# Order of the retrieval entries behind the projections: blocks 4 and 5 run their best experts into their lists, blocks 6 and 7 take theirs along with their lists

## The chip, the cores and the metric

The kernel runs on 1 core of one Trainium2 chip. The metric is the device time of one execution in microseconds. Three timed runs of the kernel before took 1407.05, 1413.61 and 1411.08 us, median 1411.08.

## The reference, cut to what matters

One decoder block over 1024 tokens of 1024 channels in float32. A gated linear attention branch and a chunked gating branch share one input projection; they are merged, projected back and added to x. Behind them stands a mixer of experts, on which the change works:

```python
h2 = modulate(rms_norm(x, norm2_w), shift2, scale2)
q = (h2 @ w_q)                        # 8 heads, two halves of 128
s1, s2 = q1 @ keys1.T, q2 @ keys2.T   # 128 scores each
v1, i1 = top_k(s1, 16); v2, i2 = top_k(s2, 16)
cand = v1[:, None] + v2[None, :]      # 256 candidates
top_s, pos = top_k(cand, 16)
idx = (i1 * 128 + i2)[pos]            # 16 of 16384 experts a head
g = softmax(top_s)
u, vv = expert_down[idx], expert_up[idx]
y2 = sum(g * gelu(u . h2) * vv)       # over 8 heads x 16 experts
x = x + gate2 * y2; out = rms_norm(x) * final_norm_w
```

## The kernel before, in words

The 1024 tokens are 8 blocks of 128, in two halves: blocks 0 to 3 and 4 to 7. For each half the kernel runs the input projections, the two branches, the output projection and the four query projections w_q(0) to w_q(3); each of these gives two of the eight heads. Large products are split into a rounded part and a rest, three products each.

**Entries.** The experts are worked off in *entries*: one entry gives each of 128 tokens one expert. Its down row and up row (1024 numbers each) are gathered from a table in memory by an indirect DMA that GpSimd (POOL) issues (gather, L524); the down row is multiplied with h2 and summed on VectorE (DVE), goes through Gelu on ScalarE (ACT) and scales the up row, which TensorE (PE) adds into an accumulator acc by a product with a diagonal matrix W. There are two kinds, told apart by the second number of an entry (b, j):

- *Direct entries*, j = 0 to 7: the best expert of head j of every token of block b. Its number is known as soon as the two tops of that head are: rank writes it for two heads at a time into a table, dix of query projection j // 2 (L1790). The dot product is one pass over 128x1024 on DVE (L537), W comes from L542 and is called Wd.
- *List entries*, j = 8 to 16: the other experts whose weight is not zero, packed over the tokens of a block. entry_list (L545) makes an entry's row by two products on PE (tps, L551 and L552) with a selection matrix E, reads the expert's number out of it on DVE (L557) and ACT (ix, L560), and then gathers. Its h2 rows come from four products (hps, L581 and L582), and its dot product is two passes over 128x512 (L583). Entry j = 17 adds rows of tokens that needed the exact search (rare_rows, L631).

**Lists.** The lists of a half are packed once, in pack_half (L300): prefix sums on DVE, then one product on PE (aux from cnt and ltri, L316), here called *the packing product*, then places, a rounded part th and a rest tl. In the second half it waits until more than PACK = 9 members stand in `behind`, a list that holds the last score product of the projections and then each add of a direct entry behind it; so nine adds are issued before it. Adds and packing product are issued in that order (queued, L601).

**The order of the entries** is a list written out by hand, todo in peer_stream (L782). seg(b, js) appends entries; unless told otherwise it opens an accumulator at its first entry and closes it at its last. There are two accumulators. A segment that closes, of a block that is not finished with it, is kept in SBUF by rows_keep (L658): a copy on ACT at the first (L663), an addition on DVE at the next (yb, L660). After 5 list entries of rare tokens and blocks 0 to 3 come, before the change:

- EARLY: heads 0 to 3 of block 5, 0 to 3 of block 6, 0 to 5 of block 7
- heads 0 to 5 of block 4; here ends stage 1
- LATER: heads 4 to 7 of block 5, 4 to 7 of block 6, 6 and 7 of block 7
- heads 6 and 7 and then the lists of block 4, the list of block 5, the rare list, the lists of blocks 6 and 7, with the rare rows of each block between

The main loop runs on beside the second half's projections. fill (L871) starts gathers up to 5 entries ahead there and 7 ahead behind them; until the projections are over it starts no entry past stage 1, and the loop stops after 12 entries (HOLD) from the start of EARLY. So 12 direct entries are added beside the projections and 20 behind them. A scheduler then places the instructions of each engine; every engine works its own queue in order.

Of the kernel before, what the change touches and what calls it, by code (L numbers as in the profile page):

```python
# [23 lines left out]
BH = HALF // P  # L24
# [8 lines left out]
PH = 8  # L33
# [21 lines left out]
PACK = 9  # L55
SHARE = 3
RP = .84
RP2 = .84
EARLY = ((5, 0, 4), (6, 0, 4), (7, 0, 6))
LOOK = 3  # L60
LATER = ((5, 4, 8), (6, 4, 8), (7, 6, 8))
HRB = (0, 1)
EB0 = 1
SQ = False
# [17 lines left out]
def block_kernel(ctx: ExitStack, tc: tile.TileContext, x, xT, cT, w_ada, b_ada, b_adaT, n1T, w_inp, w_alr,  # L82
# [114 lines left out]
    routed, weighted, summed, topped = set(), set(), set(), set()  # L197
# [584 lines left out]
    def peer_stream():  # L782
        last = PH + NT
        todo, opens, closes, runs = [], set(), set(), set()

        def seg(b, js, open_=True, close=True):
            if open_:
                opens.add((b, js[0]))
            if js[0] < PH:
                runs.add((b, js[0]))  # L790
            todo.extend((b, j) for j in js)
            if close:
                closes.add((b, js[-1]))
# [3 lines left out]
        for b in range(BH):  # L797
            seg(b, range(0 if b not in summed else PH, last + 1))
        for b, j0, j1 in EARLY:
            seg(b, range(j0, j1))  # L800
        seg(BH, range(6))
        stage1 = len(todo)
        for b, j0, j1 in LATER:
            seg(b, range(j0, j1))
        seg(BH, range(6, last))
        seg(BH + 1, range(PH, last))
        seg(NBLK + 1, range(PH, PH + NTR[1]))
        seg(BH + 2, range(PH, last - 1), close=False)
        seg(BH, (last,))
        seg(BH + 2, (last - 1, last), open_=False)  # L810
        seg(BH + 3, range(PH, PH + 3), close=False)
        seg(BH + 1, (last,))
        seg(BH + 3, (*range(PH + 3, last - 1), last, last - 1), open_=False)
        held, turn = {}, 0
# [56 lines left out]
        def fill(nxt, k):  # L871
            while nxt < len(todo):
                b, j = todo[nxt]
                if nxt > k + (AHD if len(use) == 1 and spare and j < PH else use[-1]["ahead"]):
                    break
                if len(use) == 1 and b >= BH and b != NBLK and (nxt >= stage1 or (1, j // 2) not in topped):
                    break
                lists(nxt)
                nxt += 1
            return nxt  # L880
# [3 lines left out]
        def split(k):  # L884
            if k in wvs and wvs[k] is None:
                rows_of[k] = split_rows(ents[k])

        nxt = fill(0, -1)
        yield
        nd = dots(0, -1)  # L890
# [3 lines left out]
        yield  # L894
        first, begun = todo.index((BH, PH)), todo.index(EARLY[0][:2])
        for k, (b, j) in enumerate(todo):
            if k == first - 3:
                listed.append(True)
            nxt = fill(nxt, k)
            while len(use) == 1 and k >= begun + HOLD:  # L900
                yield
                nxt = fill(nxt, k)
# [98 lines left out]
    onchip, spare, behind, listed, rared = {}, [], [], [], []  # L1001
# [54 lines left out]
    with ExitStack() as pa:  # L1056
# [339 lines left out]
        for hf in range(NHALF):  # L1396
# [203 lines left out]
            if hf == NHALF - 1:  # L1600
                qdir.drain()
                pg.close()
                use.append(peer_pools("0", "right", 3, 1, 1, 2, EB0, False))
                qp.add(peer_stream())
# [310 lines left out]
```

## Time and profile before

| what | value |
|---|---|
| timed runs, median of 3 | 1411.08 us |
| profiled execution, its own time | 1415.25 us |
| its span, first to last instruction | 1413.5 us |
| mean granted clock of TensorE | 0.98 |
| PE busy | 1342.3 us, 95% of the span |
| DVE busy | 1076.3 us, 76% |
| ACT busy | 696.3 us, 49% |
| DMA | 348.15 MB, mean 246 GB/s |

The profile is one execution. Busy time counts an engine's instructions; matmuls are pipelined, so a busy PE is not one at its peak. In the timeline a row gives start, duration, engine, line, operation, the tile written and those read; in brackets stands how long the engine sat idle before it and what ended that. The DMA share is the mean busy share of the core's 16 DMA engines.

### The profile page before, as it was taken

The page shows a single profiled execution, that of the slowest core. Times are in us where ns is not written, and L with a number is a line of the kernel's source. Part 1 is how long each engine was busy: PE and PEld are TensorE (multiplying, and loading weights), DVE is VectorE, ACT ScalarE, POOL GpSimd, SP SyncE. Part 2 cuts the span into 40 slices and gives each one's busy share as a digit, 9 for nine tenths or more (in the row PEclk, how much of TensorE's full clock was granted, in tenths as well). Part 3 has the DMA queues.
Part 4 walks back from the last instruction along what each step waited for, and adds up shares of the span by engine and source line. Part 5 has one row for each costly group of instructions (what it writes and reads, how often), then busy time and mean ns, then how long its engine had stood idle before and what let it go on. Part 6 is the DMA issues. An engine that isn't in the chain of part 4 may idle for free.

```text
span 1413.5 us, 19575 instructions
## 1 busy us (share of the span) xinstructions
PE 1342.3 (95%) x5998; PEld 1033.8 (73%) x5998; DVE 1076.3 (76%) x3066; ACT 696.3 (49%) x1568; POOL 273.7 (19%) x271
## 2 busy tenths in 40 slices
PE   8999999999999899998999999999998999888996
PEld 6678877788888878776777788778777876444553
DVE  7785778643468578798889887878889877799785
ACT  4454335433245355474544665546555545555542
POOL 0000002000000021232452132211111123453321
PEclk9999999999999999999999999999999999999998
DMA  9763556732257469757787699796588568997974
GB/s 328 244 215 113 186 161 207 236 121 89 88 175 246 149 205 324 273 148 263 234 310 267 222 363 343 269 353 241 190 314 312 193 217 322 333 418 315 383 292 190
DMA packets 123492, 348.15 MB, mean 246 GB/s; under 512 B 15385, under 2 KB 24857, under 8 KB 111346
## 3 DMA queue, kind: packets, MB, share of 16 engines
q0 software_dynamic: 31488, 163.85, 31.7%
q1 hardware_dynamic: 72240, 133.44, 28.2%
q10 hardware_dynamic: 19650, 49.54, 9.7%
q8 instruction: 48, 0.79, 0.2%
q14 instruction: 66, 0.54, 0.1%
HBM read 318.35 MB, written 28.42 MB: 245 GB/s over the span
## 4 chain that ended last, share of the span: by engine, by line
PE 41%; DVE 8%; DMA 7%; issue 5%; ACT 3%; POOL 1%; DVEq 0%; ACTq 0%; POOLq 0%
PE mm L184 6%; PE mm L185 6%; PE mm L187 6%; PE acc L609 6%; PE mm L190 2%; PE mm L191 2%; PE mm L192 2%; PE aux L1805 2%; PE hps L581 1%; PE hps L582 1%; DMA uvd<-in_down_dram,dix 1%; DMA wt<-in_w_outp_dram 1%; DMA uv<-in_tab_dram,dix 1%; PE acc L629 1%; PE acc L628 1%
## 5 line engine op out<-in xcount | busy, mean ns | idle before, releaser
L1390 ACT ACTIVATE wh<-wt 128x512 fp32r<-128x512 f32 x344 | 212.4, 628 | 273.6 <-PE mm L185 120.7
L1392 DVE TENSOR_TENSOR wl<-wt,wh 128x512 fp32r<-128x512 f32 x344 | 231.5, 684 | 119.7 <-ACT wh L1390 58.4
L184 PE MATMUL mm<-wh,hTh 128*128 128x512 f32 x648 | 255.9, 395 | 3.1 <-ACT wh L1390 3.1
L185 PE MATMUL mm<-wh,hTl 128*128 128x512 f32 x648 | 255.0, 394 | 0.0
L187 PE MATMUL mm<-wl,hTh 128*128 128x512 f32 x648 | 202.7, 396 | 0.5 <-DVE wl L1392 0.5
L184 PEld LDWEIGHTS mm<-wh,hTh 128*128 128x128 f32 x648 | 121.9, 188 | 32.1 <-ACT wh L1390 4.0
L185 PEld LDWEIGHTS mm<-wh,hTl 128*128 128x128 f32 x648 | 121.8, 188 | 26.1 <-issue 0.8
L187 PEld LDWEIGHTS mm<-wl,hTh 128*128 128x128 f32 x648 | 120.3, 188 | 27.9 <-DVE wl L1392 1.9
L528 POOL DMA_INDIRECT uv<-in_tab_dram,ix x74 | 76.8, 1038 | 267.9 <-ACT ix L560 170.8
L184 PE MATMUL mm<-hTh,wh 128*128 128x512 f32 x240 | 96.8, 403 | 0.1
L185 PE MATMUL mm<-hTl,wh 128*128 128x512 f32 x240 | 95.1, 396 | 0.0
L583 DVE SCALAR_TENSOR_TENSOR uv<-uv,hps 128x512 f32<-128x512 f32 x112 | 74.7, 680 | 20.5 <-DMA uv<-in_tab_dram,ix 11.5
L190 PE MATMUL mm<-wh,hTh 128*128 128x512 f32 x216 | 86.6, 409 | 1.0 <-DVE sg L1624 0.9
L191 PE MATMUL mm<-wl,hTh 128*128 128x512 f32 x216 | 85.3, 395 | 0.1
L192 PE MATMUL mm<-wh,hTl 128*128 128x512 f32 x216 | 85.3, 395 | 0.0
L190 PE MATMUL mm<-hTh,wh 128*128 128x256 f32 (+1 forms) x208 | 71.7, 347 | 6.5 <-DVE q L1528 5.5
L191 PE MATMUL mm<-hTl,wh 128*128 128x256 f32 (+1 forms) x208 | 70.2, 339 | 3.2 <-DVE hTl L176 3.2
L187 PE MATMUL mm<-hTh,wl 128*128 128x512 f32 x240 | 71.6, 397 | 0.0
L192 PE MATMUL mm<-hTh,wl 128*128 128x256 f32 (+1 forms) x208 | 68.8, 337 | 0.0
L609 PE MATMUL acc<-uv,W 128*128 128x512 f32 x132 | 63.1, 600 | 4.0 <-ACT W L598 3.6
L621 DVE SCALAR_TENSOR_TENSOR vl<-uv,r,vh 128x512 fp32r<-128x512 f32 x82 | 59.9, 746 | 8.5 <-ACT vh L620 5.0
L755 POOL DMA_INDIRECT uvd<-in_down_dram,dix x32 | 33.6, 1049 | 159.9 <-DVE dix L1790 40.0
(957 smaller groups left out, 2883.4 us busy)
## 6 DMA issues: line engine op xcount, KB each, us to landing
wt<-in_w_inp_dram SPq DMA_DIRECT2D x224, 256.0 KB
wt<-in_w_qp_dram SPq DMA_DIRECT2D x72, 256.0 KB
wada<-in_w_ada_dram SPq DMA_DIRECT2D x32, 512.0 KB
wt<-in_w_outp_dram SPq DMA_DIRECT2D x56, 256.0 KB
wada<-in_w_ada_dram SPq DMA_DIRECT2D x32, 256.0 KB
s_d<-so ACTq DMA_DIRECT2D x28, 256.0 KB
xt<-in_xT_dram SPq DMA_DIRECT2D x16, 256.0 KB
xr<-in_x_dram ACTq DMA_DIRECT2D x8, 512.0 KB
```

The costliest lines, as they stand in the source:

```text
L184: nc.tensor.matmul(ps, lh, rh, start=False, stop=False)
L185: nc.tensor.matmul(ps, *((lh, rl) if feat else (ll, rh)), start=False, stop=False)
L187: nc.tensor.matmul(ps, *((ll, rh) if feat else (lh, rl)), start=False, stop=False)
L190: nc.tensor.matmul(ps, lh, rh, start=first, stop=False)
L191: nc.tensor.matmul(ps, lh, rl, start=False, stop=False)
L192: return nc.tensor.matmul(ps, ll, rh, start=False, stop=last).ins
L528: nc.gpsimd.indirect_dma_start(out=dst[:], out_offset=None, in_=src, in_offset=off)
L583: nc.vector.scalar_tensor_tensor(uv[0][:, sl], uv[0][:, sl], 1.0, hps, op0=OP.mult, op1=OP.mult, accum_out=r[:, 2 + n:3 + n])
L609: ins = nc.tensor.matmul(acc[:, sl], W, v[:, sl], start=first, stop=last).ins
L621: nc.vector.scalar_tensor_tensor(vl, v, r[:, 5:6], vh.bitcast(F32), op0=OP.mult, op1=OP.subtract)
L1390: nc.scalar.activation(wh, wt, AF.Identity)
L1392: nc.vector.tensor_tensor(wl, wt, wh.bitcast(F32), op=OP.subtract)
```

## The change

```diff
--- before.py
+++ after.py
@@ -56,9 +56,8 @@
 SHARE = 3
 RP = .84
 RP2 = .84
-EARLY = ((5, 0, 4), (6, 0, 4), (7, 0, 6))
+EARLY = ((5, 0, 4), (6, 0, 4), (7, 0, 4))
 LOOK = 3
-LATER = ((5, 4, 8), (6, 4, 8), (7, 6, 8))
 HRB = (0, 1)
 EB0 = 1
 SQ = False
@@ -798,17 +797,16 @@
             seg(b, range(0 if b not in summed else PH, last + 1))
         for b, j0, j1 in EARLY:
             seg(b, range(j0, j1))
-        seg(BH, range(6))
-        stage1 = len(todo)
-        for b, j0, j1 in LATER:
-            seg(b, range(j0, j1))
-        seg(BH, range(6, last))
-        seg(BH + 1, range(PH, last))
+        stage1 = len(todo) + 6
+        seg(BH, range(PH), close=False)
+        seg(BH + 1, range(4, PH), close=False)
+        seg(BH, range(PH, last), open_=False)
+        seg(BH + 1, range(PH, last), open_=False)
         seg(NBLK + 1, range(PH, PH + NTR[1]))
-        seg(BH + 2, range(PH, last - 1), close=False)
+        seg(BH + 2, range(4, last - 1), close=False)
         seg(BH, (last,))
         seg(BH + 2, (last - 1, last), open_=False)
-        seg(BH + 3, range(PH, PH + 3), close=False)
+        seg(BH + 3, range(4, PH + 3), close=False)
         seg(BH + 1, (last,))
         seg(BH + 3, (*range(PH + 3, last - 1), last, last - 1), open_=False)
         held, turn = {}, 0
@@ -874,6 +872,8 @@
                 if nxt > k + (AHD if len(use) == 1 and spare and j < PH else use[-1]["ahead"]):
                     break
                 if len(use) == 1 and b >= BH and b != NBLK and (nxt >= stage1 or (1, j // 2) not in topped):
+                    break
+                if j >= PH and b == BH and b not in routed and len(behind) <= PACK:
                     break
                 lists(nxt)
                 nxt += 1
```

EARLY loses heads 4 and 5 of block 7, LATER is gone. Behind EARLY stand now:

- all eight heads of block 4 (stage 1 still ends six entries into them), with the accumulator left open
- heads 4 to 7 of block 5, with the other accumulator left open
- the lists of block 4 and of block 5, each into its open accumulator, then the rare list
- heads 4 to 7 of block 6 ahead of its list in one segment, and the same for block 7

So 12 entries are direct before the first list instead of 20, and the other 8 stand among the list entries. Of the nine segments of blocks 4 to 7 that closed into SBUF, four with an addition on DVE are gone. The new condition in fill keeps it from starting block 4's list, while the half isn't packed, before nine adds stand behind the projections, which is what pack_half waits for.

The instructions are the same but for those four additions; what changes is the order. On POOL, at the end of the projections, the gathers stand in this order before (uv is a whole expert, uvu and uvv its two halves; dix1_2 and dix1_3 are the tables of the third and fourth query projection of the second half):

```order
L528 DMA uv_12117<-in_tab_dram,dix1_2_139 128x2048
L528 DMA uvu_12172<-in_down_dram,dix1_2_139 128x1024
L528 DMA uvv_12173<-in_up_dram,dix1_2_139 128x1024
L528 DMA uv_12152<-in_tab_dram,dix1_3_140 128x2048
L528 DMA uv_12162<-in_tab_dram,dix1_3_140 128x2048
L528 DMA uv_12184<-in_tab_dram,dix1_2_139 128x2048
L528 DMA uv_12194<-in_tab_dram,dix1_3_140 128x2048
L528 DMA uv_12206<-in_tab_dram,dix1_3_140 128x2048
L528 DMA uvu_12261<-in_down_dram,dix1_3_140 128x1024
L528 DMA uv_12219<-in_tab_dram,dix1_3_140 128x2048
L528 DMA uvv_12262<-in_up_dram,dix1_3_140 128x1024
L528 DMA uv_12291<-in_tab_dram,dix1_3_140 128x2048
```

and after the change in this one, at the same place (lines are one lower there, and ix is the expert's number of a list entry):

```order
L527 DMA uvv_11952<-in_up_dram,dix1_2_139 128x1024
L527 DMA uvu_12130<-in_down_dram,dix1_2_139 128x1024
L527 DMA uvv_12131<-in_up_dram,dix1_2_139 128x1024
L527 DMA uv_12116<-in_tab_dram,dix1_3_140 128x2048
L527 DMA uv_12119<-in_tab_dram,dix1_3_140 128x2048
L527 DMA uv_12142<-in_tab_dram,dix1_2_139 128x2048
L527 DMA uv_12152<-in_tab_dram,dix1_3_140 128x2048
L527 DMA uv_12162<-in_tab_dram,dix1_3_140 128x2048
L527 DMA uvu_12241<-in_down_dram,ix_12239 128x1024
L527 DMA uvv_12242<-in_up_dram,ix_12239 128x1024
L527 DMA uv_12258<-in_tab_dram,ix_12256 128x2048
L527 DMA uv_12277<-in_tab_dram,ix_12275 128x2048
```

Four gathers from the fourth table are left ahead of the first list gather, where there were eight, and the first list gather is a pair of halves.

On PE, from the add ahead of the packing product to the first row of a list, before:

```order
L609 MATMUL acc_12213<-uvv_12128,Wd_12199 128x512 x2
L316 MATMUL aux_12216<-cnt_124,ltri_63 128x4
L609 MATMUL acc_12213<-uv_12141,Wd_12211 128x512 x2
L403 MATMUL aux_12248<-cnt_124,ltri_63 128x1
L609 MATMUL acc_12213<-uv_12152,Wd_12239 128x512 x2
L609 MATMUL acc_12213<-uv_12162,Wd_12286 128x512 x2
L609 MATMUL acc_12309<-uvv_12173,Wd_12296 128x512 x2
L609 MATMUL acc_12309<-uv_12184,Wd_12307 128x512 x2
L581 MATMUL hps_12549<-hh_12312,E_12323 128x512
```

and after:

```order
L608 MATMUL acc_12126<-uv_12119,Wd_12181 128x512 x2
L608 MATMUL acc_12197<-uvv_12131,Wd_12188 128x512 x2
L315 MATMUL aux_12200<-cnt_124,ltri_63 128x4
L608 MATMUL acc_12197<-uv_12142,Wd_12195 128x512 x2
L608 MATMUL acc_12197<-uv_12152,Wd_12336 128x512 x2
L608 MATMUL acc_12197<-uv_12162,Wd_12394 128x512 x2
L550 MATMUL tps_12231<-th_12213,E_12228 128x170
L551 MATMUL tps_12231<-tl_12214,E_12228 128x112
```

Two entries from the fourth table (uv_12116 and uv_12119) now stand ahead of the packing product, as the seventh and eighth add behind the projections; behind it come three direct adds and then the rows of lists, where there were eleven direct adds.

## The prediction

> **What bounds the kernel now.** I read the page first, for the shares of the whole span:
>
> ```profile
> span 1413.5 us, 19575 instructions
> PE 1342.3 (95%) x5998; PEld 1033.8 (73%) x5998; DVE 1076.3 (76%) x3066; ACT 696.3 (49%) x1568; POOL 273.7 (19%) x271
> ```
>
> TensorE (PE) is busy for 95% of the span, so the question is where its missing 5% lies. The change acts behind the second half's projections, so I then asked for the busy time of each engine there, in stretches cut at events of PE (the columns are length, then PE, weight load, DVE, ACT and POOL busy, the granted clock, the DMA share and its rate):
>
> ```profile
> 1218.30:1228.70 10.40, 10.40 (x27) 4.62 (x27) 9.54 (x46) 5.84 (x16) 3.07 (x3) 1.00 0.95 334
> 1228.70:1240.50 11.80, 7.30 (x14) 2.61 (x12) 11.73 (x65) 7.89 (x17) 9.24 (x8) 0.86 0.87 306
> 1240.50:1250.60 10.10, 10.10 (x29) 4.99 (x30) 9.78 (x34) 5.42 (x18) 3.87 (x4) 1.00 1.01 423
> 1250.60:1269.50 18.90, 14.01 (x46) 7.51 (x45) 18.58 (x76) 11.33 (x43) 11.18 (x10) 1.00 1.02 417
> 1269.50:1310.00 40.50, 36.08 (x124) 20.47 (x124) 36.58 (x192) 22.59 (x76) 14.43 (x16) 1.00 0.83 329
> 1310.00:1360.00 50.00, 48.84 (x163) 27.49 (x163) 40.21 (x158) 25.91 (x87) 17.13 (x18) 1.00 0.94 363
> 1360.00:1402.20 42.20, 40.99 (x122) 20.96 (x121) 30.87 (x98) 17.99 (x56) 9.31 (x11) 1.00 0.67 255
> ```
>
> PE idles 4.5, 4.9, 4.4, 1.2 and 1.2 us in the second, fourth, fifth, sixth and seventh stretch, 16.2 us in all. Up to 1269.5 VectorE (DVE) is full (11.73 of 11.80, 18.58 of 18.90) and the DMA too: this is the stretch of the 20 direct entries (best experts, whose index needs no list). From 1269.5 the list entries run, and PE is the bound.
>
> The timeline of PE gives the events (start, duration, line, tiles; an entry's two products show as x4, or x8 for two entries; in brackets the idle time and what ended it):
>
> ```profile
> 1218.38 1.88 PE L609 MATMUL acc<-uv,Wd 128*128 128x512 f32 x4
> 1220.10 1.88 PE L609 MATMUL acc<-uvv,Wd 128*128 128x512 f32 x4
> 1228.68 1.88 PE L609 MATMUL acc<-uv,Wd 128*128 128x512 f32 x4
> 1234.64 3.10 PE L609 MATMUL acc<-uv,Wd 128*128 128x512 f32 x4 [4.08 <-ACT Wd L542]
> 1237.54 2.50 PE L609 MATMUL acc<-uvv,Wd 128*128 128x512 f32 x4
> 1240.46 0.38 PE L316 MATMUL aux<-cnt,ltri 128*128 128x4 f32 x2 [0.43 <-DVE cnt L310]
> 1250.61 0.33 PE L551 MATMUL tps<-th,E 128*128 128x170 f32 x1
> 1266.53 1.98 PE L609 MATMUL acc<-uv,Wd 128*128 128x512 f32 x4 [1.08 <-ACT Wd L542]
> 1269.50 1.88 PE L609 MATMUL acc<-uv,W 128*128 128x512 f32 x4
> 1309.84 1.88 PE L609 MATMUL acc<-uv,W 128*128 128x512 f32 x4
> 1312.71 1.88 PE L609 MATMUL acc<-uv,W 128*128 128x512 f32 x4
> ```
>
> A direct entry takes PE 1.72 us (1218.38 to 1220.10), a list entry 2.87 (1309.84 to 1312.71). The first seven direct entries run at full pace, PE waits 4.08 us for the eighth, and after the ninth comes the packing product (L316, 1240.46), from which the lists of blocks 4 to 7 are made. From there to the first row of a list (L551, 1250.61) pass 10.15 us, and to the first list entry's add (1269.50) 29.0 us, which eleven direct entries cover.
>
> **The change part by part.** It leaves 12 of the 20 direct entries behind the projections and puts 8 (heads 4 to 7 of blocks 6 and 7) among the list entries. The sum of PE's work does not move, so the change is worth what it does to PE's idle time. I follow PE from 1218.38 to the first list add, in both orders.
>
> First gap. The change puts block 4's eight heads first. Its heads 6 and 7 take their expert numbers from the last table, dix_3, which comes from the last projection; in the order of before, the first such entry was the eleventh, now it is the seventh. These rows show when the table is written, when its first gather is issued, and how long a full gather takes (from the chain of waits, once with a short queue and once with a loaded one):
>
> ```profile
> 1229.27 0.16 DVE L1790 SCALAR_TENSOR_TENSOR dix<-ti 128x8 int32<-128x8 uint32 x1
> 1230.37 0.93 POOL L528 DMA_INDIRECT uv<-in_tab_dram,dix  x1 [0.30 <-DVE ts L362]
> 1155.97 5.20 DMA uv<-in_tab_dram,dix
> 1200.68 10.24 DMA uv<-in_tab_dram,dix
> 1264.04 1.21 DVE L537 SCALAR_TENSOR_TENSOR uv<-uv,xr 128x1024 f32<-128x1024 f32 x1
> ```
>
> Six entries are ready: PE is done with them at 1218.4 + 6 x 1.72 = 1228.7. In the new order one dot product (1.2) less stands ahead of the table, so it is written at 1228.1; the gather is issued 1.1 later (as 1230.37 is after 1229.27), at 1229.2. I take 5.2 for it, since by then the earlier gathers are through and few new ones can be issued; the loaded 10.24 is the upper end. It lands at 1234.4, the dot ends at 1235.6, and the add follows 1.3 later (1264.04 + 1.21 to 1266.53): 1236.9. The gap is 8.2 us where it was 4.08. A full gather is 128 x 2048 x 4 bytes, 1.05 MB. The Trainium skill (DMA: Bandwidth & Descriptors, Anatomy of one DMA) fits a GpSimd-issued transfer with 2.0 us plus its bytes at 436 GB/s; by that the gather would take an estimated 4.4 us, and the sum would be 0.8 lower.
>
> The packing product. It is still held until nine adds are issued, so it now stands behind heads 6 and 7 of block 4 and head 4 of block 5. Two adds after the gap run slowly, 2.9 us apart as 1234.64, 1237.54 and 1240.46 are, then 1.72: it starts at 1236.9 + 7.5 = 1244.4, 3.9 later than before. Queued behind it on DVE are the copy of its result and all that makes the lists; everything of blocks 4 to 7 waits for that. The new break in fill adds no wait of its own on an engine: it keeps lists from being recorded before this product, where there would be nothing to make them from.
>
> From the packing product to the first list add. Between 1240.4 and 1250.6 DVE's groups are
>
> ```profile
> L537 DVE SCALAR_TENSOR_TENSOR uv<-uv,xr 128x1024 f32<-128x1024 f32 x4 | 4.9, 1215 | 0.0
> L537 DVE SCALAR_TENSOR_TENSOR uvu<-uvu,xr 128x1024 f32<-128x1024 f32 x1 | 1.2, 1219 | 0.0
> L660 DVE TENSOR_TENSOR yb<-yb,acc 128x1024 f32<-128x1024 f32 x1 | 1.2, 1212 | 0.0
> ```
>
> Six passes of 1.21 start there, the last too late to delay the row. In the new order one dot is left, so four passes go: 10.15 - 4.8 = 5.3, and the first row of a list comes at 1249.7. The price of none going is 4.8 more. Then
>
> ```profile
> 1253.24 0.94 POOL L528 DMA_INDIRECT uv<-in_tab_dram,ix  x1 [7.26 <-ACT ix L560]
> 1266.71 0.68 DVE L583 SCALAR_TENSOR_TENSOR uv<-uv,hps 128x512 f32<-128x512 f32 x1
> ```
>
> The gather was issued 2.6 after the row (1250.61 to 1253.24), which I keep: 1252.3. It waited 13.5 us for its dot behind queued gathers; in the new order the queue has run dry. The first one is now a pair of half transfers, so I take 5.2 less half of 1.05 MB's 2.5 us at 417 GB/s: 3.95, with 10.24 as the upper end again. It lands at 1256.3, and 2.8 later (1266.71 to 1269.50) comes the add: 1259.1. That is 10.4 us earlier than before, but with 8 x 1.72 = 13.8 us of direct adds still to do: 3.4 us lost.
>
> The second restart. PE now has only three entries behind the packing product, done at about 1249.6, and then little until 1259.1. The two slow adds after the 4.08 us gap, under a granted clock of 0.86 in that stretch, took 3.10 + 2.50 instead of 2 x 1.88: 1.8 us more. A few list products fall into the second gap, so I take 1 us, between 0 and 1.8. The Trainium skill (TensorE: Matmul & The Clock Gate, What's actually happening) says that after an idle window of about 3.4 us the array runs at half rate until it has been busy about as long; by that each restart costs an estimated 1.7 us, and the sum would be 0.7 higher.
>
> The list stretch. As one window it reads
>
> ```profile
> 1269.50:1402.20 132.70, 125.90 (x407) 68.92 (x406) 107.66 (x447) 66.48 (x219) 40.87 (x45) 1.00 0.82 318
> ```
>
> The eight direct entries bring DVE 1.21 us each against 1.72 of PE, 70%; the stretch stands at 107.66 of 132.7, 81%. So DVE gets a little more room, and I take 1 us off the idle 6.8 (4.4, 1.2 and 1.2); at best all of it goes. The DMA moves 318 GB/s x 132.7 = 42 MB there; with eight gathers of 1.05 more in 13.8 us more it is 345 GB/s, still under the 417 to 423 of the full stretches, so I take nothing for it and up to 4 us as the upper end, since direct entries ask for a gather each 1.72 us. The four ScalarE copies of the accumulator (L663) stay. Four accumulator passes on DVE (L660) fall away, of which one was under PE's work in the list stretch; two products with g2row (L643) move under the projections' matmuls, where PE hides them; if not, 2.4 us.
>
> Sum: 3.4 + 1 - 1 = 3.4 us longer than the profiled execution, whose time is 1415.25 (span 1413.5). The three timed runs have a median of 1411.08; the difference carried over to it gives 1411.08 + 3.4 = 1414.5.
>
> **The rivals.** *Slower: the last table's gather gates everything.* Place: head 6 of block 4, seventh in line. If its gather meets a loaded queue and takes 10.24, the packing product and all lists move by 5.0 with it: 3.4 + 5.0 = 8.4, 1419.5. For it: the DMA share is 0.95 and 0.87 in the first two stretches, and PE has nothing else in its order. Against it: fewer gathers are ahead. It decides once the landing takes over 8.9 us (3.7 more, a sum past 7.1), or both gathers over 7.1.
>
> *Faster: DVE was the bound and the gathers stay hidden.* Between 1218 and 1270 DVE also has
>
> ```profile
> L660 DVE TENSOR_TENSOR yb<-yb,acc 128x1024 f32<-128x1024 f32 x3 | 3.6, 1210 | 0.0
> L643 DVE TENSOR_TENSOR yb<-yb,g2row 128x1024 f32<-128x1024 f32 x2 | 2.4, 1210 | 0.0
> ```
>
> These and eight dots (9.7) leave the stretch, 15.7 us. If the first list add moves by all of that, it comes at 1253.8; 13.8 are owed, so 1.9 are won, and with DVE's relief the idle 6.8 of the list stretch goes as well: 8.7, 1402.4. For it: DVE is full from 1228.7 to 1269.5. Against it: a gather's latency does not shrink with DVE's work. It decides if the first list add comes before about 1255.
>
> *No effect* (1411.1): the eight entries only change places and every gap is filled by others. The order of PE's rows speaks against it, with three adds behind the packing product instead of eleven.
>
> **How the numbers follow.** I give the forecast 0.47, the gated gather 0.30, the DVE case 0.18 and no effect 0.05. A measurement of this kernel can tell about 0.5% (7.1 us; its three runs differ by 6.6) from no change. The forecast and no effect are inside that: 0.52; faster 0.18, slower 0.30. The range takes in the slower rival and part of a second late gather, up to 1425, and goes down to 1404, short of the faster rival's full 1402.4.
>
> **What would show it.** Right: a gap of about 8 us before the seventh direct add, the packing product some 26 us behind the first add (22 before), a second gap of 6 to 9 us before the first list add, and that add some 41 us behind the first (51 before). Wrong: PE running from the sixth to the seventh add without a gap, a first list add under 37 us behind the first, or a list stretch whose idle time differs from 6.8 by over 4 us.

## The result and the profile after

The changed kernel takes 1425.63 us, the median of four runs (1422.19 to 1431.79), beside 1411.13 of four runs of the kernel before: a ratio of 1.0123, with a 95% interval of 1.0092 to 1.0154. It is slower by 14.5 us. Forecast were 1414.5 us, a range of 1404 to 1425, and a difference too small to tell.

The page of the profiled execution, whose own time is 1425.7 us:

```profile
span 1424.0 us, 19593 instructions
PE 1348.8 (95%) x5998; PEld 1035.5 (73%) x5998; DVE 1075.0 (75%) x3062; ACT 697.9 (49%) x1568; POOL 278.5 (20%) x272
```

The shares say nothing: TensorE is again at 95%. What moved is seen when the span is cut at events of the program. The first table of the second half (dix) is written here:

```profile
1125.14 0.17 DVE L1790 SCALAR_TENSOR_TENSOR dix<-ti 128x8 int32<-128x8 uint32 x1
```

in the kernel before, and after the change here:

```profile
1122.50 0.17 DVE L1790 SCALAR_TENSOR_TENSOR dix<-ti 128x8 int32<-128x8 uint32 x1
```

| stretch, us | before | after | difference |
|---|---|---|---|
| span's start to the first table | 1125.1 | 1122.5 | -2.6 |
| to the first direct add behind the projections | 93.2 | 88.1 | -5.2 |
| to the first list add | 51.1 | 40.0 | -11.2 |
| to the end of the last add | 132.7 | 161.5 | +28.8 |
| to the span's end | 11.3 | 11.9 | +0.6 |
| sum | 1413.5 | 1424.0 | +10.5 |

The first line is scatter between executions: in eleven of the variants below, whose instructions up to there are the changed kernel's, that table comes between 1116.8 and 1130.0. The third and fourth lines belong together, since eight direct adds of 1.72 us (13.8) moved from one to the other: the way to the first list add lost 13.8 - 11.2 = 2.6, and the list stretch lost 28.8 - 13.8 = 15.0. That is where the time went.

The timeline of TensorE after the change, from the first direct add to the first list add (start, duration, line, tiles; idle time and what ended it in brackets):

```profile
1210.58 1.88 PE L608 MATMUL acc<-uv,Wd 128*128 128x512 f32 x4
...
1227.80 6.43 PE L608 MATMUL acc<-uv,Wd 128*128 128x512 f32 x8 [6.69 <-ACT Wd L541]
...
1235.78 0.28 PE L315 MATMUL aux<-cnt,ltri 128*128 128x4 f32 x2
...
1241.29 0.39 PE L550 MATMUL tps<-th,E 128*128 128x170 f32 x1
...
1248.16 0.79 PE L580 MATMUL hps<-hh,E 128*128 128x512 f32 x1 [3.47 <-DVE uvu L582]
...
1250.55 3.56 PE L608 MATMUL acc<-uvv,W 128*128 128x512 f32 x4
```

and GpSimd's issues in the same stretch:

```profile
1219.90 0.93 POOL L527 DMA_INDIRECT uv<-in_tab_dram,dix  x1 [9.75 <-DVE ts L361]
...
1243.09 0.94 POOL L527 DMA_INDIRECT uvu<-in_down_dram,ix  x1 [17.29 <-ACT ix L559]
```

This is nearly the forecast, event by event: six adds, a gap, the packing product 25.2 us behind the first add (forecast 26), 5.5 us to the first row of a list (5.3), 1.8 to its gather (2.6), and the first list add at +40.0 (41). Only the second gap is smaller than the 6 to 9 us forecast: between the last direct add and the first list add lie 9.0 us, and list products fill 5.0 of them, so TensorE idles 4.0.

The stretches behind it (length, then busy PE, weight load, DVE, ACT, POOL, the granted clock, DMA share and rate):

```profile
1250.50:1290.00 39.50, 36.49 (x119) 19.71 (x119) 35.35 (x200) 23.45 (x76) 14.29 (x16) 0.96 0.86 333
1290.00:1354.30 64.30, 62.58 (x194) 33.32 (x193) 47.76 (x178) 32.54 (x109) 30.62 (x31) 1.00 1.02 415
1354.30:1401.50 47.20, 38.46 (x106) 18.65 (x105) 32.83 (x102) 17.10 (x57) 12.67 (x13) 0.93 0.75 291
1401.50:1412.10 10.60, 10.57 (x29) 5.08 (x27) 3.62 (x12) 2.97 (x9) 0.00 (x0) 1.00 0.10 41
```

TensorE idles 3.0, 1.7, 8.7 and 0.0 us, 13.5 in all where it was 6.8, and the granted clock, 1.00 throughout before, costs another 0.04 x 39.5 + 0.07 x 47.2 = 4.9. These are 11.6 of the 15.0 us; the other 3.4 lie in busy time and could not be placed. The worst piece is the third, in which the DMA has room (0.75) and TensorE, VectorE and ScalarE all idle. Its timeline:

```profile
1356.21 1.94 PE L608 MATMUL acc<-yrk,Wr 128*128 128x512 f32 x4
...
1360.76 0.50 PE L580 MATMUL hps<-hh,E 128*128 128x512 f32 x1 [2.44 <-DVE uvu L582]
...
1362.45 3.25 PE L608 MATMUL acc<-uvv,W 128*128 128x512 f32 x4 [0.36 <-ACT W L597]
...
1371.35 1.96 PE L608 MATMUL acc<-uv,Wd 128*128 128x512 f32 x4 [3.28 <-ACT rd L539]
```

and VectorE at the same time:

```profile
1356.76 0.28 DVE L556 SCALAR_TENSOR_TENSOR jk<-ts__13488,slot 128x56 f32<-128x56 f32 x1 [1.75 <-ACT ts__13488 L553]
...
1357.16 1.22 DVE L643 TENSOR_TENSOR yrv<-yrv,yb 128x1024 f32<-128x1024 f32 x1
...
1358.49 1.22 DVE L704 TENSOR_TENSOR yr<-acc,g2row 128x1024 f32<-128x1024 f32 x1
...
1360.01 0.68 DVE L582 SCALAR_TENSOR_TENSOR uvu<-uvu,hps 128x512 f32<-128x512 f32 x1
...
1361.23 1.22 DVE L705 TENSOR_TENSOR yr<-yr 128x1024 f32<-128x1024 f32 x1
...
1363.76 0.15 DVE L170 TENSOR_SCALAR fs<-fs 128x1 f32<-128x1 f32 x1 [1.12 <-ACT yr L709]
1364.60 1.28 DVE L712 SCALAR_TENSOR_TENSOR yr<-yr,fs,fw 128x1024 f32<-128x1024 f32 x1 [0.69 <-POOL fs L171]
1365.81 1.22 DVE L536 SCALAR_TENSOR_TENSOR uv<-uv,xr 128x1024 f32<-128x1024 f32 x1
...
1370.03 1.22 DVE L704 TENSOR_TENSOR yr<-acc,g2row 128x1024 f32<-128x1024 f32 x1
```

L704 to L712 finish a block: the rows from 1358.49 to 1364.60 are block 4's, L704 at 1370.03 is block 6's, and L643 prepares block 5's. They stand between the dot products (L582, L536). VectorE itself waits there, 1.75 us for a list's row (L556), 1.12 for ScalarE's sum of squares (L170) and 0.69 for GpSimd's power (L712).

TensorE's two long waits are for passes in that queue. The 2.44 us are for the dot product at 1360.01, whose h2 product had been done at 1354.5. The 3.28 us are for block 6's L704: block 7's first add goes into the accumulator that block 6 has just left, and it starts at 1371.35, 0.10 us behind the end of L704. The view names ScalarE's L539, but that had ended at 1370.67, and the semaphore records of the trace hold TensorE's queue until 1371.29 for a count of VectorE's, raised at 1371.26. In e4, e6, e11 and e15 the add that waits at this place starts 0.10 to 0.15 us behind the same pass, too. Whether this is the cause or only a place where a shortage shows, the experiments had to tell.

### The profile page after: what moved, and what is told of

Read it like the earlier page. It is cut to its first block, busy times and chain, and to the rows that moved or that the text cites. A ratio compares the mean times of both kernels' runs of the same rounds, so it can differ in the third digit from the quotient of the medians.

```text
span 1424.0 us, 19593 instructions
## 1 busy us (share of the span) xinstructions
PE 1348.8 (95%) x5998; PEld 1035.5 (73%) x5998; DVE 1075.0 (75%) x3062; ACT 697.9 (49%) x1568; POOL 278.5 (20%) x272
## 5 line engine op out<-in xcount | busy, mean ns | idle before, releaser
L582 DVE SCALAR_TENSOR_TENSOR uv<-uv,hps 128x512 f32<-128x512 f32 x110 | 72.9, 682 | 28.1 <-DMA uv<-in_tab_dram,ix 12.7
L580 PE MATMUL hps<-hh,E 128*128 128x512 f32 x128 | 63.3, 495 | 12.1 <-DVE uvu L582 5.9
```

Of the source, the lines that this page charges most:

```text
L580: nc.tensor.matmul(hps, Ej, hh[:, sl], start=True, stop=False)
L582: nc.vector.scalar_tensor_tensor(uv[0][:, sl], uv[0][:, sl], 1.0, hps, op0=OP.mult, op1=OP.mult, accum_out=r[:, 2 + n:3 + n])
```

## The experiments

Beside each run stands its ratio to the kernel before on the same chip, with its 95% interval. 0.001 is 1.4 us. "Add to add" is the time from the first direct add behind the projections to the end of the last add, 183.8 us before and 201.5 after.

### Which part of the change: e1, e2, e3

```diff
 # e1: both lines added, and both lists start at PH again; e2: block 6 alone; e3: block 7 alone
         seg(BH, range(PH), close=False)
+        seg(BH + 2, range(4, PH))
+        seg(BH + 3, range(4, PH))
         seg(BH + 1, range(4, PH), close=False)
...
-        seg(BH + 2, range(4, last - 1), close=False)
+        seg(BH + 2, range(PH, last - 1), close=False)
...
-        seg(BH + 3, range(4, PH + 3), close=False)
+        seg(BH + 3, range(PH, PH + 3), close=False)
```

> The changed kernel with heads 4 to 7 of blocks 6 and 7 put back ahead of the lists (behind head 7 of block 4, ahead of heads 4 to 7 of block 5); blocks 4 and 5 still run into their lists. So 20 direct entries stand ahead of the first list entry, as before the change. Theory A (too little cover ahead of the lists; every four direct entries ahead count alike): all of the loss comes back, 1409 to 1413 us. Theory B (the four of block 7, late in the list stretch, collide there with the finishing of blocks 4 and 5 on VectorE): the same, 1409 to 1413, since they are ahead here too. Theory C (heads 6 and 7 of block 4 stand seventh in line and wait for the last table, and the packing product behind them): that place is kept, so 1420 to 1426.

Measured: 1411.86 us, 1.0011 (0.9987 to 1.0035). All of the loss is gone; theory C, the late table ahead of the packing product, falls.

> The changed kernel with only block 6's heads 4 to 7 put back ahead of the lists; block 7's stay with its list. Theory A: half of the 14.5 us comes back, about 1418. Theory B: block 7's four are what costs, so 1422 to 1426. Theory C: 1422 to 1426.

Measured: 1416.94 us, 1.0048 (1.0022 to 1.0075).

> The changed kernel with only block 7's heads 4 to 7 put back ahead of the lists; block 6's stay with its list. Theory A: half comes back, about 1418. Theory B: 7 to 10 us come back, the idle time and slow clock between 1357 and 1371 in the changed kernel's profile: 1415 to 1418, and in its profile TensorE has no gap of over 2 us around the finishing of block 4. Theory C: 1422 to 1426. With the two runs beside it: if six ahead and seven ahead each bring as much as the other, it is A, if seven ahead brings nearly all, B.

Measured: 1419.44 us, 1.0059 (1.0036 to 1.0083). Each four bring about half, whichever block they belong to. That is what theory A expected, though why they count is not shown by it; B in its first form, in which block 7's four alone were to blame, falls. Running blocks 4 and 5 into their lists costs nothing that can be told.

### Is the packing product late: e4

```diff
-PACK = 9
+PACK = 6
```

> The changed kernel with the packing product held for six adds instead of nine: it then stands ahead of the seventh add and its wait for the last table. Its operand (the counts) was written 7.7 us before the packing product started in the changed kernel's profile (1227.8 against 1235.8). If the wait for the packing product costs what it lasts, the first list add comes 7 us earlier and the time is 1417 to 1419. If the list stretch is bound by its own gathers or by VectorE, the start moves but the end does not: 1423 to 1426.

Measured: 1425.37 us, 1.0119 (1.0084 to 1.0153): no gain. The profile shows what the product then waits for:

```profile
1233.22 0.56 PE L315 MATMUL aux<-cnt,ltri 128*128 128x4 f32 x2 [7.00 <-DVE cnt L309]
...
1251.68 3.49 PE L608 MATMUL acc<-uvv,W 128*128 128x512 f32 x4 [0.34 <-ACT W L597]
```

It starts 17.5 us behind the first add instead of 25.2, the first list add comes at +35.9 instead of +40.0, and add to add the profiled execution takes 195.4. So the first list add comes 4.1 us earlier, not 7, and the timed runs show neither these 4 nor the 6 us of the profiled execution; in their interval of 0.7% this stays open.

### Thin start or the entries themselves: e5, e6, e7

```diff
 # e5: the eight entries left out
-        seg(BH + 2, range(4, last - 1), close=False)
+        seg(BH + 2, range(PH, last - 1), close=False)
...
-        seg(BH + 3, range(4, PH + 3), close=False)
+        seg(BH + 3, range(PH, PH + 3), close=False)
```

> The changed kernel with heads 4 to 7 of blocks 6 and 7 left out altogether (eight direct entries of the 384 or so are not computed). The stretch from the first to the last list add took 161.5 us in the changed kernel, 147.7 without eight direct adds of 1.72, and 132.7 before the change. Theory L (lead: with 12 entries ahead the list entries start with too few gathers on their way, whatever stands among them later): it stays at 145 to 148, and the time is 1425.6 - 13.8 = about 1412. Theory D (the moved entries themselves: among list entries each needs its gather of 1.05 MB, 2.5 us at 417 GB/s, beside a DMA that is full there, so that it costs more than its 1.72 us of TensorE): the stretch falls to 131 to 136, and the time is 1396 to 1401.

Measured: 1414.54 us, 1.0011 (0.9983 to 1.0039). (The kernel has 64 direct entries, 8 heads in 8 blocks, not 384.) The profiled execution, the slowest of the ten, has nearly 8 us behind the last add that belong to none of the theories (the last section); whether the others have them is not known, so I read the stretches. The list stretch:

```profile
1258.00:1399.20 141.20, 132.06 (x412) 70.04 (x411) 109.34 (x473) 69.10 (x227) 46.50 (x50) 0.98 0.85 322
```

141.2 us lies between the two theories. Of the 15.0 us, 141.2 - 132.7 = 8.5 remain without the eight entries, so they come with a start that has only 12 entries ahead; the other 6.5 come with the entries. This rests on one execution of each kernel.

```diff
 # e6
-    def gather(ul, ix):
+    def gather(ul, ix, half=False):
         uv = pair(ul, "uv")
         off = bass.IndirectOffsetOnAxis(ap=ix, axis=0)
+        if half:
+            nc.gpsimd.indirect_dma_start(out=uv[0][:], out_offset=None, in_=down, in_offset=off)
+            return [uv[0], uv[0]]
...
-        return pl, b, h, h2, r, gather(ul, dcol(dixq, b, h))
+        return pl, b, h, h2, r, gather(ul, dcol(dixq, b, h), b >= BH + 2 and h >= 4)
```

> The changed kernel with the gathers of those eight entries (heads 4 to 7 of blocks 6 and 7) halved: only the down row is gathered, and the add uses it in place of the up row. All instructions of TensorE, VectorE and ScalarE stay; 8 x 0.52 MB fewer are moved, 10 us of DMA at 417 GB/s. Theory D: 6 to 10 us come back, 1415.5 to 1420. Theory L: under 2 us, 1423.5 to 1426.

Measured: 1431.93 us, 1.0174 (1.0125 to 1.0223), the profiled one again with 8 to 9 us more behind the last add; add to add 199.8, 1.7 less than the changed kernel. Ten microseconds less of DMA bring under two: theory D falls, though the DMA share was 1.02 for 64 us.

```diff
 # e7
-        seg(BH + 2, range(4, last - 1), close=False)
+        seg(BH + 2, (PH, 4, PH + 1, 5, PH + 2, 6, PH + 3, 7, *range(PH + 4, last - 1)), close=False)
...
-        seg(BH + 3, range(4, PH + 3), close=False)
+        seg(BH + 3, (PH, 4, PH + 1, 5, PH + 2, 6, PH + 3, 7), close=False)
...
-        seg(BH + 3, (*range(PH + 3, last - 1), last, last - 1), open_=False)
+        seg(BH + 3, (*range(PH + 4, last - 1), last, last - 1), open_=False)
...
-                if (b, j) in runs:
+                if (b, j) in runs or b not in h2s:
```

> The changed kernel with the eight entries spread: in blocks 6 and 7 a list entry stands between each two of heads 4 to 7, instead of four in a row ahead of the list. If four in a row are what costs (four dot products and four gathers at once, in the profile a wait of 3.3 us of TensorE ahead of block 7's four), 5 to 8 us come back: 1418 to 1421. Theories L and D alone: 1423 to 1428.

Measured: 1429.89 us, 1.0153 (1.0115 to 1.0190), add to add 202.2. Four in a row are not the cost.

### Is it the number of gathers ahead: e10, e11

```diff
-AH = 7
+AH = 8    # e11: 6
```

> The changed kernel with gathers started up to 8 entries ahead behind the projections instead of 7. Theory L (each list entry's round from its row over gather, dot product and weight to its add takes longer than 7 entries of TensorE's work, so what is on its way bounds the list stretch when it starts thin): the stretch shortens by 4 to 8 us, 1418 to 1422. If the number on its way does not bound (the order of work on VectorE and ScalarE does): within 2 us of the changed kernel's 1425.6.

Measured: 1425.31 us, 1.0118 (1.0092 to 1.0144).

> The changed kernel with 6 entries ahead instead of 7. Theory L: 6 to 12 us slower, 1432 to 1438. Otherwise within 2 us of 1425.6.

Measured: 1425.85 us, 1.0117 (1.0084 to 1.0150). Neither one more nor one fewer changes anything. Theory L keeps its observation (8.5 us come with the thin start) and loses its mechanism.

### Twenty ahead, in a better order: e9, e12, e8

```diff
 # e9: e1 with block 7's four ahead of block 6's, and heads 6 and 7 of block 4 last
-        seg(BH, range(PH), close=False)
+        seg(BH, range(6), close=False)
+        seg(BH + 3, range(4, PH))
+        seg(BH + 2, range(4, PH))
         seg(BH + 1, range(4, PH), close=False)
-        seg(BH, range(PH, last), open_=False)
+        seg(BH, range(6, last), open_=False)
...         # both lists start at PH, as in e1
```

> All twenty direct entries ahead of the lists and blocks 4 and 5 merged as in the run with both ahead (1411.9), with heads 6 and 7 of block 4 last, behind heads 4 to 7 of blocks 7, 6 and 5: the order is block 4 heads 0 to 5, then 7, 6, 5, then 6 and 7 of block 4 and its list. The first entry that needs the last table is now ninth instead of seventh, so TensorE's gap there falls from 6.7 to about 3.5 us. If that gap is on the path, 1408 to 1410. If the gathers of the list entries set the pace from there on, 1411 to 1413.

Measured: 1407.82 us, 0.9981 (0.9954 to 1.0009); add to add 184.4:

```profile
1206.30:1260.20 53.90, 43.24 (x112) 20.20 (x111) 49.47 (x224) 28.17 (x85) 30.54 (x27) 0.94 0.97 373
1260.20:1390.70 130.50, 126.05 (x407) 69.09 (x405) 105.26 (x438) 67.54 (x220) 41.41 (x44) 1.00 0.86 329
```

The list stretch is back at 130.5 with 4.5 idle. With 12 ahead and eight left out (e5), add to add took 180.4. Eight entries ahead thus cost 4.0 us, 0.5 each, since they run in waits that are there anyway; in e1, which differs from e5 in these eight alone, add to add took 187.6, so 0.9 each. In the list stretch they cost 201.5 - 180.4 = 21.1, 2.6 each.

> The run with twenty entries ahead and block 4's heads 6 and 7 last (0.9981 of the kernel before), with 8 entries ahead instead of 7. There TensorE waits for little in the list stretch (3.9 us), so theory L gives at most 2 us: 0.996 to 0.999 of the kernel before.

Edit: e9 with `AH = 8`. Measured: 1412.37 us, 1.0012 (0.9993 to 1.0031). No gain.

```diff
 # e8: e9's idea with the old EARLY
-EARLY = ((5, 0, 4), (6, 0, 4), (7, 0, 4))
+EARLY = ((5, 0, 4), (6, 0, 4), (7, 0, 6))
...
-        seg(BH, range(PH), close=False)
+        seg(BH, range(6), close=False)
+        seg(BH + 2, range(4, PH))
+        seg(BH + 3, range(6, PH))
         seg(BH + 1, range(4, PH), close=False)
-        seg(BH, range(PH, last), open_=False)
+        seg(BH, range(6, last), open_=False)
...         # both lists start at PH, as in e1
```

> Twenty direct entries ahead, blocks 4 and 5 merged into their lists, but with the old EARLY (heads 4 and 5 of block 7 in it, right behind the twelve entries that run beside the projections); heads 4 to 7 of block 6, 6 and 7 of block 7, 4 to 7 of block 5 and 6 and 7 of block 4 follow block 4's heads 0 to 5. From the first table's writing to the first direct add behind the projections 93.2 us passed before the change and 87.9 to 88.6 in the changed kernel and its variants. If it is heads 4 and 5 of block 7 at that place (their table is the third) that held the projections' end up, this run shows 92 to 94 and is about 5 us slower than the same order with the new EARLY (0.9981): 1.001 to 1.002. If it is the merging, 88 and 0.998.

Measured: 1412.43 us, 1.0027 (1.0002 to 1.0051). From the first table to the first direct add pass 92.4 us, as expected if heads 4 and 5 of block 7 at that place hold the projections' end up; in e9 it was 89.0.

### VectorE: e13, e14, e15, e17

```diff
 # e13 (changed kernel), e14 (e9)
+                if n == 0 or not pl["own"]:
                     nc.vector.scalar_tensor_tensor(uv[0][:, sl], uv[0][:, sl], 1.0, hps, op0=OP.mult, op1=OP.mult,
                                                    accum_out=r[:, 2 + n:3 + n])
...         # the Gelu takes the first sum in place of the second
```

> The changed kernel with the second of the two dot-product passes of each list entry of the second half left out (the entry's sum over channels 512 to 1023 is not computed); TensorE's work and the gathers stay. VectorE is relieved of about 0.6 us in each of some 41 list entries, 25 us in all. Theory V (TensorE and VectorE go in step in the list entries, since the h2 products need two PSUM tiles that the dot products must free, so each other pass on VectorE that falls there delays TensorE; ahead of the lists VectorE idles in the two waits and what it could have done there comes later): 8 to 16 us come back, 1410 to 1418, and it gains at least 5 us more than the same edit gives the order with twenty entries ahead. If VectorE is not what delays: under 3 us.

Measured: 1417.25 us, 1.0059 (1.0040 to 1.0078): 0.0064 under the changed kernel, 9 us (add to add 194.8, 6.7 less).

> The same edit in the order with twenty entries ahead and block 4's heads 6 and 7 last (0.9981 of the kernel before). Its list stretch idles TensorE for 3.9 us only, so 1 to 5 us come off: 0.994 to 0.998. Theory V: less than the edit gives the changed kernel. If the gain is the same in both, VectorE's load is not what tells the two orders apart.

Measured: 1409.19 us, 0.9998 (0.9979 to 1.0016), beside 0.9981 of e9 without the edit: nothing gained. The same relief brings 9 us in the one order and none in the other. That is what theory V expected. The edit takes two things away, though: 25 us of VectorE's time, and the wait for the second of the two h2 tiles, which nothing reads any more. VectorE's time as a whole is not short: in e14's list stretch it is busy for 82.03 of 130.7 us, in the changed kernel's for 119.6 of 161.6, a smaller share than before the change (107.66 of 132.7).

```diff
 # e15 (changed kernel), e17 (e9); in rare_rows the passes of L642 and L643 go for these two blocks as well
     def finish(pl, b, acc, part=False):
...
+        if b in (BH, BH + 1):
+            nc.scalar.activation(y, acc, AF.Identity)
+            nc.sync.dma_start(out[0, b * P:(b + 1) * P, :], y)
+            yield
+            return
```

> The changed kernel without the finishing of blocks 4 and 5 (their ten full-width passes on VectorE, with the wait for GpSimd's power between them, are replaced by one copy on ScalarE and the store; these two blocks' outputs are not computed to the end). In the changed kernel's profile TensorE falls back by about 11 us from 1354 to 1401, where block 4 and 5 are finished and block 7's four direct entries stand. Theory F (the finishing passes hold up block 7's dot products there): 7 to 12 us come back, 1414 to 1419. If they only fill VectorE's idle time: under 3 us.

Measured: 1418.80 us, 1.0064 (1.0039 to 1.0089): 8 us back (add to add 191.9, 9.6 less). The list stretch falls from 161.6 to

```profile
1254.40:1406.60 152.20, 143.77 (x444) 75.66 (x443) 108.27 (x477) 75.59 (x248) 55.63 (x57) 0.99 0.89 354
```

and around block 4's end the wait of 2.44 us is gone (the add behind it waits 1.21), and that of 3.28 becomes 1.36.

> The edit of the run without the finishing of blocks 4 and 5 (their outputs are not computed to the end), made in the order with twenty entries ahead and block 4's heads 6 and 7 last (0.9981 of the kernel before). In the changed kernel it brought 8 us. If the finishing passes are a cost of their own in any order, it brings 6 to 9 us here too: 0.992 to 0.994. If they hurt only where TensorE has no slack ahead of VectorE, as in the changed kernel, it brings 0 to 3 us: 0.996 to 0.999.

Measured: 1408.57 us, 0.9993 (0.9964 to 1.0021), beside 0.9981: nothing. The finishing passes cost 8 us in the changed order and none that can be told in e9's. In the kernel before they are there too, nearer to the end by some 20 us (1368 to 1402.2, where it is 1358.5 to 1412.1 after the change), and the same steps of block 4 show no wait of VectorE for ScalarE or GpSimd:

```profile
1367.95 1.23 DVE L705 TENSOR_TENSOR yr<-acc,g2row 128x1024 f32<-128x1024 f32 x1 [0.75 <-PE acc L609]
...
1370.70 1.22 DVE L706 TENSOR_TENSOR yr<-yr 128x1024 f32<-128x1024 f32 x1
...
1373.90 0.14 DVE L171 TENSOR_SCALAR fs<-fs 128x1 f32<-128x1 f32 x1
...
1375.57 1.22 DVE L706 TENSOR_TENSOR yrv<-yrv,yru 128x1024 f32<-128x1024 f32 x1
1376.71 1.28 DVE L713 SCALAR_TENSOR_TENSOR yr<-yr,fs,fw 128x1024 f32<-128x1024 f32 x1
```

L171 and L713 run without a bracket: dot products and another block's passes lie between each step and the next, so that the sum of squares and the power are done when VectorE comes to them.

### More ahead, and a better version: e16, e18

> The order with twenty entries ahead and block 4's heads 6 and 7 last (0.9981), with 8 instead of 12 direct entries beside the projections, so 24 stand behind them. If direct entries ahead of the first list entry are nearly free there, because they run in a wait that is there anyway (from first direct add to last add 180.4 us with 12 ahead and eight left out, 184.4 with 20: 0.5 us each), the projections end 4 x 1.72 = 6.9 us earlier and 2 us are given back: 0.993 to 0.996. If the wait is full at 20, four more cost 6.9 and nothing is won: 0.997 to 1.001.

Edit: e9 with `HOLD = 8`. Measured: 1419.03 us, 1.0067 (1.0049 to 1.0084). The projections do end 7 us earlier (82.1 from the first table, 89.0 in e9), but add to add takes 189.9, 5.5 more than with 20 where the four adds take 6.9, and the profiled run has 9 us more behind its last add. Without those it would be level with the kernel before: at 20 the wait is nearly full.

> The best order so far (twenty entries ahead, block 4's heads 6 and 7 last, 0.9981 with an interval that holds 1) with the packing product held for eight adds instead of nine, so that it stands ahead of the first add that waits for the last table. If the lists' start sets that order's pace, 2 to 3 us come off, 0.995 to 0.997, and it beats both kernels; if not, 0.997 to 1.000.

Edit: e9 with `PACK = 8`. Measured: 1411.18 us, 1.0012 (0.9990 to 1.0033). No order tried beats the kernel before by more than its interval; e9 comes nearest.

## Why the prediction was wrong

**The first gap and the packing product: right.** The gap was 6.69 us (8.2 forecast), since the table came 8.3 us behind the first add, not 9.7; its gather took from 1219.90 to 1225.5, 5.6 us (5.2), so the rival of the gated gather (8.9 and more) did not occur. Its other condition, "both gathers over 7.1", should have read 6.4, as the second was taken at 3.95 and not at 5.2; that one took 4.3. The two adds behind the gap ran slowly, 6.43 us for both.

**To the first list add: right.** +40.0 (41). The loss up to there is 2.6 us, where the sum had 3.4. The second gap was 4.0 us of idle time, not 6 to 9, for list products ran in it. The faster rival needed this add before 1255 on the old clock, 37 us behind the first, and fell.

**The projections' end: not in the sum.** I costed at nothing what the change does there, and it gained 5.2 us. Before, VectorE waited there for gathers, and TensorE's last scores for the copy of the queries on ScalarE (waits between 1195.7 and 1218.3, total, times and longest):

```profile
DVE uv L537 <- DMA uv<-in_tab_dram,dix: 5.1, 2, 2.6
DVE uvu L537 <- DMA uvu<-in_down_dram,dix: 1.6, 1, 1.6
...
PE aux L1805 <- ACT qt L1756: 2.1, 2, 1.1
```

After the change neither wait is among the rows of that stretch, whose only wait of TensorE is

```profile
PE aux L1805 <- ACT so L1807: 0.5, 1, 0.5
```

e8 ties it to heads 4 and 5 of block 7 in EARLY: with them back, the 92.4 us are back.

**The list stretch: here the prediction failed.** The step read: the eight entries bring VectorE 1.21 us each against 1.72 of TensorE, less than the stretch's share, so VectorE gets more room; "I take 1 us off the idle 6.8". It lost 15.0 us, and its idle time went from 6.8 to 13.5 us, where the prediction had named a difference of over 4 as a sign of being wrong. The step reckoned with shares of busy time, and by shares it was right: VectorE's share did fall. It left out that two engines which work in turns wait for each other's queues. An entry's h2 products fill two PSUM tiles (the pool hps has two), which the dot products must free before TensorE can go on; a block's first add needs an accumulator, which a finishing pass of another block must have read. What stands ahead of these in VectorE's queue is handed on to TensorE. TensorE's longest waits in the list stretch (total, times and longest) were before

```profile
PE acc L609 <- ACT W L598: 5.2, 6, 1.7
PE hps L581 <- DVE uv L583: 0.9, 3, 0.3
```

and after the change

```profile
PE acc L608 <- ACT W L597: 4.0, 11, 0.6
PE acc L608 <- ACT rd L539: 3.3, 1, 3.3
PE hps L580 <- DVE uv L582: 3.0, 5, 1.1
PE hps L580 <- DVE uvu L582: 2.4, 1, 2.4
```

The waits for dot products grew from 0.9 to 5.4 us, and the 3.3 are the wait for block 6's pass; with 1.2 less for ScalarE's weights this is 6.6 of the 6.7 us of added idle time. In e9 the waits for dot products come to 1.0.

Shown is thus that TensorE waits for passes in VectorE's queue in the changed order, and hardly in the order of before and in e9's. Taking work out of that queue, either 25 us of passes or the two finishings, brings 8 to 9 us with the eight among the list entries (e13, e15) and nothing that can be told with the eight ahead (e14, e17), where TensorE idles only 4.5 us and little was left to gain. Not tested is the hand-over by itself: no run had a third tile in hps, or the same passes in another order. Not shown is why e9's order escapes: the runs do not tell whether the scheduler's order of the passes there or the older lead of the gathers does it. The 8.5 us of the thin start (e5) are a measured size without a mechanism: the lookahead is not it (e10, e11). None of the prediction's rivals had this mechanism; its chance of 0.30 for slower stood on the last table's gather, which did not come late.

**The terms I did allow for.** I took up to 4 us for the DMA at the upper end. The DMA got full (1.02 from 1290 to 1354), and TensorE idled 1.7 us there; halved gathers brought under 2 (e6). The slow clock of a restart, taken at 1 us for the second gap, came twice more in the list stretch; the three cost 4.9 us there.

**The sum.** 2.6 to the first list add, 15.0 in the list stretch and 0.6 at the end, less 5.2 gained ahead and 2.6 of scatter, make the +10.5 of the profiled executions (0.1 is rounding), where 3.4 was forecast. The medians differ by 14.5, 4.0 more: the kernel before was profiled in an execution 4.1 us above its median, the changed one at its median. How these 4 us spread over the stretches is not known; the first stretch alone scatters by 13.

## What to carry to other kernels

Work that is ready early is worth more ahead of a wait than behind it: eight entries cost 0.5 to 0.9 us each as cover for the routing and 2.6 each where no wait was left to fill. When work is moved into a stretch that seems bound by one engine, ask not only whether the other engines' shares leave room, but which of their queues that engine waits on in turn, and what else stands in those queues. And give a stretch that has never been seen with the new mix a bound on both sides: mine went to +4 on the DMA's account alone.

## What the runs showed of the hardware that I had not expected

**A slow clock in pieces of one length.** Windows cut where the granted clock changes, and some ahead of them (the clock is the column behind the bracketed counts):

```profile
1226.50:1233.33 6.83, 5.53 (x7) 2.34 (x8) 5.01 (x13) 3.35 (x12) 0.00 (x0) 0.50 1.01 427
1246.98:1253.81 6.83, 5.65 (x12) 3.46 (x12) 4.86 (x21) 2.69 (x9) 4.07 (x5) 0.50 0.99 366
1359.63:1363.04 3.41, 1.92 (x6) 0.94 (x7) 3.01 (x11) 1.83 (x6) 0.93 (x1) 1.00 0.98 377
1363.04:1366.45 3.41, 3.41 (x7) 1.67 (x6) 2.00 (x3) 1.01 (x3) 0.56 (x1) 0.50 0.83 320
1366.45:1369.87 3.42, 1.62 (x4) 0.38 (x2) 3.42 (x11) 1.80 (x7) 0.00 (x0) 1.00 0.40 161
1393.76:1397.17 3.41, 2.00 (x7) 0.74 (x6) 3.41 (x9) 1.11 (x4) 0.53 (x1) 1.00 0.94 327
1397.17:1400.58 3.41, 3.41 (x5) 1.34 (x6) 2.68 (x8) 2.02 (x5) 0.55 (x1) 0.50 0.36 147
```

From the first direct add to the last add of the changed kernel the clock is halved four times, for 3.41 us or twice that, and the starts lie 6, 40 and 50 times 3.41 us behind the first. The Trainium skill (TensorE: Matmul & The Clock Gate, What's actually happening) gives an idle window of about 3.4 us, free-running, as what throttles. The length and the grid agree with it here. A window idle from end to end was not needed: in the two that stand just ahead of the later slow pieces TensorE was busy for 1.92 and 2.00 us, and the one from 1366.45, with 1.62, was not followed by a slow clock. So neither the longest idle time (2.44 us ahead of the third slow piece, 3.28 at 1371.35 ahead of none) nor the busy share orders them, and what does is open.

**Microseconds behind the last store.** From the last store's issue to the end of the span pass 7.0 us in the changed kernel (1416.99 to 1424.0). In e5 it is 14.5 us (1404.12 to 1418.6), in e6 and e16 15.6 and 15.3. The instructions at the program's end show where it goes. The longest of GpSimd's three DRAIN instructions (ns: shortest, median, longest) is in the changed kernel

```profile
L1911 POOLq DRAIN  x3: 40/107/800, 1420.0 to 1423.7; - x3
```

and in e5

```profile
L1911 POOLq DRAIN  x3: 40/107/8722, 1409.1 to 1418.3; - x3
```

It takes 0.7 to 0.9 us in seventeen profiles and 8.7 to 9.3 in e5, e6 and e16, and the other engines wait for it. From the last add's end to the span's end it is 19 to 21 us in these three, and 11.3 to 12.0 in all the others. Why GpSimd takes longer there is open; a time that has it is not compared without the stretches.
